# Layer A of a hybrid encoder: the keys of four late blocks selected in one series of small steps, spread over a half pass of the feed-forward

## The chip, the core and the metric

The kernel runs on one core of a Trainium2 chip. The metric is the device time of one execution in microseconds; lower is better. Before the change it is 2746.65 us, the median of 3 runs (2744.76 to 2747.51).

## What is computed

The input is one sequence of 1024 tokens of 1024 values in float32. Layer A is sparse attention with a feed-forward behind it, layer B is attention on a shared latent with a feed-forward behind it. In layer A an indexer scores every key for every token, and a token attends to its 256 best keys (`n_top` is 256 here). Cut to what matters:

```python
score = jnp.einsum('bqh,bqhs->bqs', wib * (IDX_HEADS ** -0.5), jax.nn.relu(dots))
score = jnp.where(admiss[None], score, NEG)
_, idx = lax.top_k(score, n_top)
...
logits = jnp.einsum('bqhd,bqkd->bhqk', qb, kg) * (A_HEAD_DIM ** -0.5) + bias
p = jax.nn.softmax(jnp.where(valid, logits, NEG))
...
def sq_relu_mlp(h, w_up, w_down):
    return jnp.square(jax.nn.relu(h @ w_up)) @ w_down
```

## The kernel before

The tokens lie in eight blocks of 128 (`tb` 0 to 7). A block sees keys up to its own end, so block `tb` has `(tb + 1) * 128` scores per token. Blocks 0 and 1 have at most 256 keys and need no selection; blocks 2 and 3 are selected early, blocks 4 to 7 late.

**Selection** (`select`, line 427) finds the 256th best score by bits: VectorE counts how many scores of a row reach a candidate threshold (line 442, one `tensor_scalar` with an accumulator for each block), compares the counts with 256 (`ok`, line 444), keeps the candidate where enough scores reach it (`thr`, line 455), and sets the next bit (`cand`, line 453). That is a sign step and 31 bits, 32 rounds for each pair of blocks, then one mask step per block (lines 461 to 467; one of its operations, line 463, runs on GpSimd). Each round of a pair is one step of a list; the steps are dealt out between other work by `weave`.

**The feed-forward** (`mlp`) runs in half passes of four blocks. A half pass has eight chunks of four slices of 128 hidden values. For each slice TensorE does 24 matmuls of 512 columns into `pu` (line 1112); ScalarE applies relu and square in place and casts the high half `hh`; VectorE subtracts to make the low half `hl` (line 86). Then 24 matmuls for each of the four blocks add up in `pd` (line 1182), and VectorE adds `pd` to `res` (line 1183). So a chunk has 192 matmuls, four `hl` and four `res`. The weights are split in the same way: ScalarE casts `uh` and `dh`, GpSimd subtracts for `ul` and `dl`, eight such splits in a chunk. `pu` has four banks, `pd` two buffers.

The first half pass (blocks 1, 3, 0, 2) carries the selection of the late blocks as its `extra` steps, first the pair 4, 5 and then the pair 6, 7 (`more` in `layer_a`). After it comes the attention of the blocks 7, 4, 5, 6, then the second half pass with those blocks, whose `extra` steps prepare the down projections of layer B (`down_weights`).

**What sets the order.** Every engine runs its instructions in the order in which a scheduler has placed them, by times that it estimates. An extra step is only kept behind an anchor: `behind` puts its instructions after a given one on the same engine. In `mlp` the anchors are those of the last transposition of the input:

```python
                anchors = turn(late[-1])
            ...
            weave(sum((chunk(c) for c in range(1, NC)), []), extra(st), lambda e: self.behind(e, anchors))
```

**The start.** `bias_table` (line 402) makes a row of position biases for each head, `brow`, and writes it 128 times to memory in `near_d`, from which the attention loads its bias tiles. `brow` lies in the tag `rel`, a ring of three buffers in which also the squares of the norm, the one-hot table, `kvt`, `kiw` and then the normalised keys `k2` (cast `k`, line 271) follow each other. The gain row of the norm has a buffer of its own, tag `gain`, which the scratch of the early selection takes over.

Of the kernel before, what the change touches and what calls it, by code (L numbers as in the profile page):

```python
# [10 lines left out]
F32 = mybir.dt.float32  # L11
F32R = mybir.dt.float32r
U32 = mybir.dt.uint32
AF = mybir.ActivationFunctionType
ALU = mybir.AluOpType
# [3 lines left out]
P = 128  # L19
# [23 lines left out]
class Trunk:  # L43
# [83 lines left out]
    def layer_a(self, res):  # L127
# [4 lines left out]
        with ExitStack() as st_a:  # L132
# [12 lines left out]
            with ExitStack() as st_p:  # L145
# [66 lines left out]
                def load_q(c):  # L212
                    ws["q", c] = weights(256 * c, 256, f"q{c}")

                ws = {}
                with ExitStack() as st_i:
# [114 lines left out]
                    near_d = self.bias_table(i2, pp)  # L331
# [21 lines left out]
                    for tb in (2, 3):  # L353
# [8 lines left out]
                          woven(early[2] + turns[2] + early[3], queries + [lambda: load_q(2)]), sel[:28])  # L362
# [11 lines left out]
                def start(turn):  # L374
                    steps = [lambda c=c, tp=tp: project_q(c, tp) for tp in (0, 2) for c in (2, 3)]
                    weave(steps[:2] + [turn] + steps[2:], sel[28:])
                    st_x.close()
# [5 lines left out]
            def more(st):  # L383
                sp = st.enter_context(tc.tile_pool(name="asel", bufs=2))
                scratch = [self.select_scratch(sp, T, "4", bufs=1)]
                return self.select((4, 5), score, sp, scratch) + self.select((6, 7), score, sp, scratch)
# [15 lines left out]
    def bias_table(self, bp, pp):  # L402
# [11 lines left out]
        row = bp.tile([16, 384], F32, name="brow", tag="rel", bufs=3, padded_shape=[16, T])  # L414
# [9 lines left out]
    def select(self, tbs, score, pool, scratch):  # L424
# [14 lines left out]
        def count():  # L439
            for j, tb in enumerate(tbs):  # L440
                s = score[tb]
                nc.vector.tensor_scalar(scratch[0][0][:, :s.shape[-1]], s, cand[:, j:j + 1], None, op0=ALU.is_ge, op1=ALU.add,  # L442
                                        accum_out=cnt[:, j:j + 1])
            nc.vector.tensor_scalar(ok, cnt, TOP, None, op0=ALU.is_ge)

        def sign():
            nc.vector.memset(cand, 0.0)
            count()
            nc.vector.tensor_copy(thr.bitcast(U32), bits[:, 32:33].to_broadcast([P, n]))
            nc.vector.copy_predicated(thr, ok, cand)  # L450

        def bit(b):
            nc.vector.tensor_tensor(cand.bitcast(U32), thr.bitcast(U32), bits[:, b:b + 1].to_broadcast([P, n]), op=ALU.bitwise_xor)
            count()
            nc.vector.copy_predicated(thr, ok, cand)

        def mask(j):
            s = score[tbs[j]]
            S = s.shape[-1]
            rank, g = (x[:, :S] for x in scratch[0])  # L460
            nc.vector.tensor_scalar(g, s, thr[:, j:j + 1], None, op0=ALU.is_gt, op1=ALU.add, accum_out=cnt[:, j:j + 1])
            nc.vector.tensor_scalar(need[:, j:j + 1], cnt[:, j:j + 1], -BIG, TOP * BIG, op0=ALU.mult, op1=ALU.add)
            nc.gpsimd.tensor_scalar(g, g, BIG, -BIG, op0=ALU.mult, op1=ALU.add)
            nc.vector.tensor_scalar(s, s, thr[:, j:j + 1], BIG, op0=ALU.is_equal, op1=ALU.mult)
            nc.vector.tensor_tensor_scan(rank, s, s, 0.0, ALU.add, ALU.bypass)
            nc.vector.scalar_tensor_tensor(rank, rank, need[:, j:j + 1], s, op0=ALU.is_le, op1=ALU.mult)
            nc.vector.tensor_add(s, rank, g)

        return [sign] + [lambda b=b: bit(b) for b in range(30, -1, -1)] + [lambda j=j: mask(j) for j in range(n)]
# [594 lines left out]
    def mlp(self, layer, res, tbs, finish, done, out=None, extra=lambda st: [], side="left"):  # L1064
# [12 lines left out]
        with ExitStack() as st:  # L1077
# [37 lines left out]
            with tc.tile_pool(name=f"ms{nm0}", bufs=2, side=side) as sp:  # L1115
# [41 lines left out]
                anchors = turn(late[-1])  # L1157
# [44 lines left out]
            weave(sum((chunk(c) for c in range(1, NC)), []), extra(st), lambda e: self.behind(e, anchors))  # L1202
# [48 lines left out]
```

## Time and profile before

| | us |
|---|---|
| median of 3 runs | 2746.65 (2744.76 to 2747.51) |
| the profiled execution | 2747.70 |
| its span | 2745.90 |
| TensorE busy | 2563.0 (93%) |
| VectorE busy | 1574.5 (57%) |
| ScalarE busy | 1236.6 (45%) |
| GpSimd busy | 1018.6 (37%) |

The profile is of one execution. Its engines are PE (TensorE; PEld is its weight loads), DVE (VectorE), ACT (ScalarE), POOL (GpSimd) and SP (which issues the DMAs). PEclk is the granted clock of TensorE as a share of full speed. Where an instruction waited, the row ends with the idle time before it and with what ended the wait.

### The profile page before, as it was taken

What the parts mean: (1) busy time and instruction counts of PE and PEld (TensorE: products, weight loads), DVE (VectorE), ACT (ScalarE), POOL (GpSimd) and SP (SyncE); (2) the same over time, 40 slices, a digit from 0 to 9 for tenths busy, and PEclk for the clock granted to TensorE, in tenths of its full rate; (3) what the DMA queues carried; (4) which work ended last, traced back from release to release, by engine and by line L of the source; (5) the groups of instructions that cost most, each with busy time, mean ns of one, the idle gap of its engine ahead of it and who ended that gap; (6) DMA issues with size and microseconds to landing.
All of it is one profiled execution on the core that took longest, in us unless ns stands there. A gap on an engine that the chain in (4) does not pass through costs nothing.

```text
span 2745.9 us, 37099 instructions
## 1 busy us (share of the span) xinstructions
PE 2563.0 (93%) x13354; PEld 2165.7 (79%) x13354; DVE 1574.5 (57%) x3888; ACT 1236.6 (45%) x2989; POOL 1018.6 (37%) x756
## 2 busy tenths in 40 slices
PE   6798888989999999999989799999999999999999
PEld 5697777767777887888879688887778888888887
DVE  5598768999729885111236888888532232222223
ACT  3476653322328764324235688888422222122221
POOL 1235643443527534435321555555212212122220
PEclk9898999999999999999999899999999999999999
DMA  6211332221323214323220000001401111111111
GB/s 145 46 40 43 92 97 77 92 92 62 108 85 91 61 42 152 110 79 123 75 60 4 12 13 9 14 7 41 138 16 46 47 46 50 43 62 42 51 46 62
DMA packets 122295, 173.05 MB, mean 63 GB/s; under 512 B 12752, under 2 KB 101104, under 8 KB 122112
## 3 DMA queue, kind: packets, MB, share of 16 engines
q1 hardware_dynamic: 122112, 170.69, 20.2%
q8 instruction: 105, 1.72, 0.3%
q14 instruction: 78, 0.64, 0.1%
HBM read 159.13 MB, written 11.53 MB: 62 GB/s over the span
## 4 chain that ended last, share of the span: by engine, by line
PE 69%; DVE 17%; DMA 4%; ACT 4%; POOL 2%; issue 2%; SPq 0%; POOLq 0%; ACTq 0%; DVEq 0%
PE pd L1182 23%; PE pu L1112 21%; DVE both L442 4%; PE pwo L1058 4%; PE blps L930 2%; PE pwoa L1058 2%; PE bpo L954 2%; PE puq L788 2%; PE pq L183 2%; PE po L566 2%; PE ppt L560 1%; PE lps L537 1%; PE bpt L949 1%; DMA near_d<-brow 1%; PE pukv L744 1%
## 5 line engine op out<-in xcount | busy, mean ns | idle before, releaser
L86 POOL TENSOR_TENSOR dl<-rd,dh 128x1024 fp32r<-128x1024 f32 x96 | 231.2, 2417 | 754.3 <-ACT dh L86 384.9
L1183 DVE TENSOR_TENSOR res<-res,pd 128x1024 f32<-128x1024 f32 x192 | 234.4, 1221 | 417.4 <-PE pd L1182 417.4
L1182 PE MATMUL pd<-dh,hl 128*128 128x512 f32 x1024 | 397.1, 394 | 28.5 <-DVE hl L86 28.5
L1112 PE MATMUL pu<-mxh,uh 128*128 128x512 f32 (+1 forms) x1056 | 408.5, 387 | 2.4 <-DVE mxl L86 2.4
L1112 PE MATMUL pu<-mxh,ul 128*128 128x512 f32 (+1 forms) x1056 | 407.8, 386 | 0.0
L1112 PE MATMUL pu<-mxl,uh 128*128 128x512 f32 (+1 forms) x1056 | 407.6, 386 | 0.0
L1182 PE MATMUL pd<-dh,hh 128*128 128x512 f32 x1024 | 399.8, 391 | 5.4 <-ACT hh L86 4.5
L1182 PE MATMUL pd<-dl,hh 128*128 128x512 f32 x1024 | 399.9, 391 | 0.0
L86 ACT CAST dh<-rd 128x1024 fp32r<-128x1024 f32 x96 | 99.1, 1052 | 483.5 <-PE pd L1182 424.7
L86 DVE TENSOR_TENSOR hl<-pu,hh 128x512 fp32r<-128x512 f32 (+1 forms) x132 | 88.8, 674 | 388.0 <-ACT hh L86 388.0
L86 POOL TENSOR_TENSOR ul<-ru,uh 128x1024 fp32r<-128x1024 f32 x96 | 232.2, 2421 | 177.6 <-ACT uh L86 154.1
L1169 ACT ACTIVATE pu<-pu 128x512 f32<-128x512 f32 (+1 forms) x132 | 75.1, 569 | 456.8 <-PE pu L1112 451.3
L1182 PEld LDWEIGHTS pd<-dh,hl 128*128 128x128 f32 x1024 | 193.8, 190 | 72.1 <-DVE hl L86 32.1
L1112 PEld LDWEIGHTS pu<-mxh,uh 128*128 128x128 f32 x1056 | 201.5, 191 | 42.5 <-DVE mxl L86 2.9
L1112 PEld LDWEIGHTS pu<-mxh,ul 128*128 128x128 f32 x1056 | 201.4, 191 | 39.7
L1112 PEld LDWEIGHTS pu<-mxl,uh 128*128 128x128 f32 x1056 | 201.0, 190 | 39.5
L1182 PEld LDWEIGHTS pd<-dh,hh 128*128 128x128 f32 x1024 | 193.2, 189 | 47.2 <-ACT hh L86 5.7
L1182 PEld LDWEIGHTS pd<-dl,hh 128*128 128x128 f32 x1024 | 193.2, 189 | 40.0
L442 DVE TENSOR_SCALAR_CACHE_REDUCE both<-score,cand 128x384 f32<-128x384 f32 (+2 forms) x192 | 181.3, 944 | 4.8
L936 POOL TENSOR_SCALAR bpr<-bpr,bsm 128x640 f32<-128x640 f32 (+7 forms) x128 | 97.7, 768 | 110.7 <-DVE bsm L935 33.3
L548 POOL TENSOR_SCALAR lg<-lg,sm 128x256 f32<-128x256 f32 (+7 forms) x128 | 98.9, 781 | 65.4 <-DVE sm L547 43.1
L86 ACT CAST uh<-ru 128x1024 fp32r<-128x1024 f32 x96 | 99.9, 1044 | 27.4 <-DMA ru<-in_mlp_w_up_dram 26.4
(384 smaller groups left out, 6062.9 us busy)
## 6 DMA issues: line engine op xcount, KB each, us to landing
ru<-in_mlp_w_up_dram SPq DMA_DIRECT2D x48, 1024.0 KB, 5.5
rd<-in_mlp_w_down_dram SPq DMA_DIRECT2D x48, 1024.0 KB, 4.9
bm<-near_d SPq DMA_DIRECT2D x56, 256.0 KB, 2.8
res<-in_x_dram SPq DMA_DIRECT2D x16, 512.0 KB, 5.3
wor_a<-in_a_w_o_dram SPq DMA_DIRECT2D x16, 512.0 KB, 3.7
wr_q<-in_a_w_in_dram SPq DMA_DIRECT2D x8, 512.0 KB, 3.8
x<-res SPq DMA_DIRECT2D x8, 512.0 KB, 2.6
wor_b<-in_b_w_o_dram SPq DMA_DIRECT2D x8, 512.0 KB, 3.7
```

The lines of the kernel that those rows point to most:

```text
L86: return self.nc.scalar.copy(h, src), (engine or self.nc.vector).tensor_sub(l, src, h)
L183: nc.tensor.matmul(out, a[x][:, kb, t0:t0 + P], b[:, kb, :], start=(kb == 0 and i == 0), stop=(kb == KB - 1 and i == 2))
L442: nc.vector.tensor_scalar(scratch[0][0][:, :s.shape[-1]], s, cand[:, j:j + 1], None, op0=ALU.is_ge, op1=ALU.add, accum_out=cnt[:, j:j + 1])
L548: nc.gpsimd.tensor_scalar(lg[:, :S], lg[:, :S], rs, 1.0, op0=ALU.mult, op1=ALU.mult)
L566: nc.tensor.matmul(po, vv[:, s0 + u], m[:, u], start=(s0 + u == 0 and n == 0), stop=(s0 + u == nb - 1 and n == 1))
L788: nc.tensor.matmul(ps[:, 192 * u:192 * u + 192], a[:, kb, tsl], b[:, kb], start=(kb == 0 and i == 0), stop=(kb == 2 and i == 2))
L936: nc.gpsimd.tensor_scalar(pr, pr, sm[:, 3:4], 1.0, op0=ALU.mult, op1=ALU.mult)
L1058: nc.tensor.matmul(open_ps[n], x[:, kb], w[:, kb, ns], start=(kb == 0 and i == 0), stop=(kb == KB - 1 and i == 2))
L1112: nc.tensor.matmul(pu, a[:, kb], b[:, kb, c0:c1], start=(kb == 0 and i == 0), stop=(kb == KB - 1 and i == 2))
L1169: nc.scalar.activation(pu, pu, AF.Relu)
L1182: nc.tensor.matmul(pd[:, ns], a[:, tsl], b[:, ns], start=(f == 0 and k == 0), stop=(f == NS - 1 and k == 2))
L1183: nc.vector.tensor_add(res[:, tb], res[:, tb], pd)
```

## The change

`select` no longer makes one step of a round but one of each count: a step is one bit of one block. The last block's step also makes `ok` and `thr`, the first block's the next `cand`. A mask is three steps. The four late blocks are one series, in the order 7, 4, 5, 6, so that `ok`, `thr` and `cand` are made once for four blocks; a sixth as many empty steps are added behind, so that the series ends ahead of the half pass. `mlp` ties an extra step to `self.tail`, the newest `hh` and `hl`, instead of to the transposition. The early selection of blocks 2 and 3 has the same steps in halves. And `brow` moves from the ring `rel` to the buffer `gain`.

```diff
-                    near_d = self.bias_table(i2, pp)
+                    near_d = self.bias_table(i2, pp, ip)
...
-                          woven(early[2] + turns[2] + early[3], queries + [lambda: load_q(2)]), sel[:28])
+                          woven(early[2] + turns[2] + early[3], queries + [lambda: load_q(2)]), sel[:56])
...
-                    weave(steps[:2] + [turn] + steps[2:], sel[28:])
+                    weave(steps[:2] + [turn] + steps[2:], sel[56:])
...
-                return self.select((4, 5), score, sp, scratch) + self.select((6, 7), score, sp, scratch)
+                steps = self.select((7, 4, 5, 6), score, sp, scratch)
+                return steps + [lambda: None] * (len(steps) // 6)
...
-        row = bp.tile([16, 384], F32, name="brow", tag="rel", bufs=3, padded_shape=[16, T])
+        row = rp.tile([16, 384], F32, name="brow", tag="gain", bufs=1, padded_shape=[16, D])
...
+        def bit(b, j):
+
+            if j == 0 and b < 0:
+                nc.vector.memset(cand, 0.0)
+                nc.vector.tensor_copy(thr.bitcast(U32), bits[:, 32:33].to_broadcast([P, n]))
+            elif j == 0:
+                nc.vector.tensor_tensor(cand.bitcast(U32), thr.bitcast(U32), bits[:, b:b + 1].to_broadcast([P, n]), op=ALU.bitwise_xor)
+            count(j)
+            if j == n - 1:
+                nc.vector.tensor_scalar(ok, cnt, TOP, None, op0=ALU.is_ge)
+                nc.vector.copy_predicated(thr, ok, cand)
...
-        return [sign] + [lambda b=b: bit(b) for b in range(30, -1, -1)] + [lambda j=j: mask(j) for j in range(n)]
+        steps = [lambda b=b, j=j: bit(b, j) for b in (-1, *range(30, -1, -1)) for j in range(n)]
+        return steps + [lambda j=j, part=part: mask(j, part) for j in range(n) for part in range(3)]
...
-                anchors = turn(late[-1])
+                self.tail = turn(late[-1])
...
-            weave(sum((chunk(c) for c in range(1, NC)), []), extra(st), lambda e: self.behind(e, anchors))
+            weave(sum((chunk(c) for c in range(1, NC)), []), extra(st), lambda e: self.behind(e, self.tail))
```

**On VectorE, in the first half pass.** `hl0_1_c_f` is the low half of slice f of chunk c, `score4` to `score7` are the scores of the late blocks. Before, from `hl` of slice 3 of chunk 1 on:

```order
L86 TENSOR_TENSOR hl0_1_1_3_5043<-pu0_1_1_3_0_5044,hh0_1_1_3_5042 128x512
L442 TENSOR_SCALAR both4_4872,cnt4_4875<-score5_80,cand4_4874 128x768
L444 TENSOR_SCALAR ok4_4876<-cnt4_4875 128x2
L455 COPY_PREDICATED thr4_4873<-ok4_4876,cand4_4874 128x2
L453 TENSOR_TENSOR cand4_4874<-thr4_4873,bits_67 128x2
L442 TENSOR_SCALAR both4_4872,cnt4_4875<-score4_79,cand4_4874 128x640
```

Four more rows like these, the rest of another round, follow ahead of the next `hl`. Now, from `hl` of slice 3 of chunk 3 on:

```order
L86 TENSOR_TENSOR hl0_1_3_3_5654<-pu0_1_3_3_0_5655,hh0_1_3_3_5653 128x512
L451 TENSOR_TENSOR cand7_4874<-thr7_4873,bits_67 128x4
L442 TENSOR_SCALAR both4_4872,cnt7_4875<-score7_82,cand7_4874 128x1024
L442 TENSOR_SCALAR both4_4872,cnt7_4875<-score4_79,cand7_4874 128x640
L442 TENSOR_SCALAR both4_4872,cnt7_4875<-score5_80,cand7_4874 128x768
L442 TENSOR_SCALAR both4_4872,cnt7_4875<-score6_81,cand7_4874 128x896
L86 TENSOR_TENSOR hl0_1_4_0_5832<-pu0_1_4_0_0_5833,hh0_1_4_0_5831 128x512
L454 TENSOR_SCALAR ok7_4876<-cnt7_4875 128x4
```

A round now counts four blocks and has its three small operations once, over four columns; rounds are cut by the `hl` of the feed-forward, and the series runs from chunk 1 into chunk 6, where the pairs ran from chunk 0 into chunk 5.

**On ScalarE, at the start.** `k_0` and `k_1` are the two halves of the normalised keys, `wr_qi_0_797` is the third load for the indexer; in brackets stand the semaphores waited for. Before, the first cast of the keys waited for the DMA that reads `brow`:

```order
L305 CAST qs__529<-pqi_256_530 64x256
L271 CAST k_0_524<-krow_508 128x4x64 [waits DMAHW3_49,DVE_49]
L271 CAST k_0_524<-krow_508 128x4x64
L247 COPY kiw<-pkv_445 72x512 [waits PE_49]
L248 CAST kih<-pkv_445 64x512
```

Now it waits for an earlier DMA, that of the one-hot table, and stands ahead of the second `kvt`; the cast of the third load still stands ahead of the second half of the keys:

```order
L271 CAST k_0_524<-krow_508 128x4x64 [waits DMAHW1_49,DVE_49]
L271 CAST k_0_524<-krow_508 128x4x64
L244 COPY kvt<-pkv_445 128x512 [waits PE_49]
L304 CAST qs__529<-pqi_256_530 64x256 [waits PE_49]
```

```order
L264 ACTIVATE ksq_596<-krow_597 128x256 [waits Activation_49]
L86 CAST wh_qi_796<-wr_qi_0_797 128x8x128 [waits DMAHW4_49]
L304 CAST qs__529<-pqi_256_646 64x256 [waits PE_49]
L305 CAST qs__529<-pqi_256_646 64x256
L271 CAST k_1_613<-krow_597 128x4x64 [waits DVE_49]
```

The last five rows read the same in both orders.

## Rows read from the trace of the kernel before

**Rows 1.** The page, part 1: busy time, share of the span, instructions.

```profile
PE 2563.0 (93%) x13354; PEld 2165.7 (79%) x13354; DVE 1574.5 (57%) x3888; ACT 1236.6 (45%) x2989; POOL 1018.6 (37%) x756
```

**Rows 2.** Windows, the two half passes: start:end length, busy us (instructions), clock, DMA.

```profile
core 0: us, PE busy (x) PEld busy (x) DVE busy (x) ACT busy (x) POOL busy (x), PEclk, DMA share, GB/s
425.70:815.50 389.80, 357.80 (x1534) 292.02 (x1532) 314.98 (x544) 115.05 (x162) 155.05 (x67) 0.96 0.25 84
1056.00:1403.80 347.80, 343.44 (x1534) 284.27 (x1533) 78.81 (x83) 122.72 (x179) 148.61 (x62) 1.00 0.30 100
```

**Rows 3.** Waits of TensorE, 425.7 to 815.5: us in total, times, longest.

```profile
PE pd L1182 <- DVE hl L86: 28.5, 7, 8.1
```

**Rows 4.** Windows, one chunk of each half pass.

```profile
522.00:575.00 53.00, 49.41 (x213) 40.50 (x212) 50.69 (x88) 14.72 (x20) 23.68 (x10) 0.97 0.25 80
1111.00:1154.00 43.00, 43.00 (x191) 35.61 (x190) 7.29 (x8) 14.49 (x20) 18.57 (x9) 1.00 0.31 100
```

**Rows 5.** Timeline of ScalarE at the start: start, length, instruction [idle before <-releaser].

```profile
73.94 0.71 ACT L271 CAST k<-krow 128x256 fp32r<-128x256 f32 x2 [18.12 <-DMA near_d<-brow]
...
79.45 0.37 ACT L86 CAST vv<-pk 128x256 fp32r<-128x256 f32 x1
...
89.00 0.71 ACT L271 CAST k<-krow 128x256 fp32r<-128x256 f32 x2 [2.96 <-DVE krow L268]
```

**Rows 6.** DMA issues, 30 to 90: count, KB each, us to landing.

```profile
near_d<-brow SPq DMA_DIRECT2D x1, 3072.0 KB, 34.2
...
wr_qi<-in_a_w_in_dram SPq DMA_DIRECT2D x1, 512.0 KB, 4.0
```

**Rows 7.** Windows, the end of the start.

```profile
66.00:92.00 26.00, 10.34 (x57) 8.96 (x56) 9.03 (x22) 11.50 (x22) 8.02 (x4) 0.64 0.48 89
```

**Rows 8.** Timeline of VectorE, one round where no split runs.

```profile
456.96 0.88 DVE L442 TENSOR_SCALAR_CACHE_REDUCE both<-score,cand 128x640 f32<-128x640 f32 x1
...
457.88 1.01 DVE L442 TENSOR_SCALAR_CACHE_REDUCE both<-score,cand 128x768 f32<-128x768 f32 x1
...
458.94 0.17 DVE L444 TENSOR_SCALAR ok<-cnt 128x2 uint32<-128x2 f32 x1
459.14 0.16 DVE L455 COPY_PREDICATED thr<-ok,cand 128x2 f32<-128x2 uint32 x1
```

**Rows 9.** Lines by form, VectorE, 425 to 800: count | busy us, mean ns | idle.

```profile
L442 DVE TENSOR_SCALAR_CACHE_REDUCE both<-score,cand 128x1024 f32<-128x1024 f32 x32 | 40.9, 1277 | 0.8
L442 DVE TENSOR_SCALAR_CACHE_REDUCE both<-score,cand 128x896 f32<-128x896 f32 x32 | 36.6, 1145 | 1.0
...
L442 DVE TENSOR_SCALAR_CACHE_REDUCE both<-score,cand 128x768 f32<-128x768 f32 x32 | 32.4, 1011 | 1.0
L444 DVE TENSOR_SCALAR ok<-cnt 128x2 uint32<-128x2 f32 x64 | 31.3, 489 | 1.5
L455 DVE COPY_PREDICATED thr<-ok,cand 128x2 f32<-128x2 uint32 x62 | 29.5, 475 | 2.1
L442 DVE TENSOR_SCALAR_CACHE_REDUCE both<-score,cand 128x640 f32<-128x640 f32 x32 | 28.1, 879 | 1.0
...
L453 DVE TENSOR_TENSOR cand<-thr,bits 128x2 uint32<-128x2 uint32 x62 | 25.0, 403 | 2.1
```

**Rows 10.** Timeline of GpSimd, VectorE and ScalarE at 492: a round that meets a split.

```profile
492.01 2.41 POOL L86 TENSOR_TENSOR dl<-rd,dh 128x1024 fp32r<-128x1024 f32 x1 [1.99 <-ACT dh L86]
...
492.46 1.99 DVE L444 TENSOR_SCALAR ok<-cnt 128x2 uint32<-128x2 f32 x1
...
494.01 0.59 ACT L86 CAST hh<-pu 128x512 fp32r<-128x512 f32 x1
```

**Rows 11.** Lines, GpSimd, 425.7 to 725: the splits.

```profile
L86 POOL TENSOR_TENSOR ul<-ru,uh 128x1024 fp32r<-128x1024 f32 x25 | 61.4, 2460 | 52.1 <-ACT uh L86 51.8
L86 POOL TENSOR_TENSOR dl<-rd,dh 128x1024 fp32r<-128x1024 f32 x25 | 60.8, 2445 | 107.4 <-ACT dh L86 107.4
```

**Rows 12.** Line 442, all counts: min/median/max ns, first and last start in us.

```profile
L442 DVE TENSOR_SCALAR_CACHE_REDUCE both<-score,cand x192: 604/942/1282, 122.2 to 713.7; 128x384 f32<-128x384 f32 x32, 128x512 f32<-128x512 f32 x32, 128x640 f32<-128x640 f32 x32, 128x768 f32<-128x768 f32 x32
```

**Rows 13.** Timeline of TensorE: the transposes of the second half of the keys.

```profile
65.90 0.60 PE L257 MATMUL pk<-ident,kvt 128*128 128x128 f32 x4
```

More of the change, by code (lines that the diff above doesn't have):

```diff
@@ L400, in gain_qk, with bias_table @@
         return gk
-    def bias_table(self, bp, pp):
+    def bias_table(self, bp, pp, rp):
         nc, tc = self.nc, self.tc
@@ L437, in select, with count, mask @@
         bits = self.bits
[L439 to L457, printed above, removed]
+        def count(j):
+            s = score[tbs[j]]
+            nc.vector.tensor_scalar(scratch[0][0][:, :s.shape[-1]], s, cand[:, j:j + 1], None, op0=ALU.is_ge, op1=ALU.add,
+                                    accum_out=cnt[:, j:j + 1])
+        def bit(b, j):
[8 more added lines that the diff above has]
+                nc.vector.copy_predicated(thr, ok, cand)
+        def mask(j, part):
             s = score[tbs[j]]
@@ L460, in mask @@
             rank, g = (x[:, :S] for x in scratch[0])
[L461 to L467, printed above, removed]
-        return [sign] + [lambda b=b: bit(b) for b in range(30, -1, -1)] + [lambda j=j: mask(j) for j in range(n)]
+            if part == 0:
+                nc.vector.tensor_scalar(g, s, thr[:, j:j + 1], None, op0=ALU.is_gt, op1=ALU.add, accum_out=cnt[:, j:j + 1])
+                nc.vector.tensor_scalar(need[:, j:j + 1], cnt[:, j:j + 1], -BIG, TOP * BIG, op0=ALU.mult, op1=ALU.add)
+                nc.gpsimd.tensor_scalar(g, g, BIG, -BIG, op0=ALU.mult, op1=ALU.add)
+                nc.vector.tensor_scalar(s, s, thr[:, j:j + 1], BIG, op0=ALU.is_equal, op1=ALU.mult)
+            elif part == 1:
+                nc.vector.tensor_tensor_scan(rank, s, s, 0.0, ALU.add, ALU.bypass)
+            else:
+                nc.vector.scalar_tensor_tensor(rank, rank, need[:, j:j + 1], s, op0=ALU.is_le, op1=ALU.mult)
+                nc.vector.tensor_add(s, rank, g)
+        steps = [lambda b=b, j=j: bit(b, j) for b in (-1, *range(30, -1, -1)) for j in range(n)]
+        return steps + [lambda j=j, part=part: mask(j, part) for j in range(n) for part in range(3)]
     def attend_a(self, tbs, res, kh, kl, vv, score, edge, near_d, wst, lp=None, start=None, beside=None, free=None):
```

## The prediction, made before the changed kernel ran

> **What bounds the kernel now.** I read the page first, then the stretches, then single lines. The page has TensorE busy for 93% of the span and VectorE for 57% [rows 1], so TensorE bounds the whole, and the question is where it is held up. Two stretches matter here. The first is the first half pass of layer A's feed-forward. The two half passes of it do the same matmuls (1534 in each stretch), so one prices the other: from the last split of the input to the last addition the first takes 389.8 us and the second 347.8 us, at a granted clock of 0.96 and 1.00 [rows 2]. The reader is to see that the difference, 42.0 us, is the most that any new order of the first half pass can give, unless it went faster than the second one, where TensorE is busy 343.4 of 347.8 us. In the first, VectorE is busy 315.0 of 389.8 us against 78.8, and what TensorE waits for is `hl`, the low half of the hidden values, which VectorE makes: 28.5 us in seven waits [rows 3]. A chunk (192 matmuls) shows it: VectorE is busy 50.7 of 53.0 us while a chunk of the second half pass takes some 43 us, with 7.3 us of VectorE [rows 4]. So here VectorE is the bound, and the selection of keys is its load.
>
> The second stretch is the start. ScalarE stands still for 18.1 us until the write of `near_d` has landed, before it can cast the normalised keys `k`; `near_d` takes 34.2 us [rows 5, 6]. In the 26 us from 66 to 92 TensorE is busy for 10.3 us, at a clock of 0.64 [rows 7].
>
> **Part 1: the series of four blocks.** Removed: per bit there was an `ok`, a `thr` and a `cand` for two blocks at a time, 64 triples; now there is one triple for all four, 32. The counts stay: 32 for each block. Their price is start to start in a quiet stretch: 0.92 us for 640 columns, 1.06 for 768, and 0.20 for each small operation [rows 8]. That is 0.04 to 0.05 us over the means, 0.88 and 1.01 us [rows 9], so I take 1.19 and 1.33 us for 896 and 1024 columns (means 1.15 and 1.28). A bit of four blocks is 4.50 + 0.60 = 5.1 us where nothing disturbs it.
>
> The small operations are not always 0.17 us: when GpSimd runs a split of weights (2.4 us) they last until it ends. At 492.0 the first of two such splits begins, and an `ok` right behind it takes 1.99 us [rows 10]; the counts stay at their 0.88 and 1.01 us. Over the stretch the small ones average 0.489, 0.475 and 0.403 us [rows 9]: over 0.165 us that is 64 x 0.32 + 62 x 0.31 + 62 x 0.24 = 54.6 us of holding, or 0.85 us per triple, or 54.6 / 50 = 1.09 us per split (25 + 25 until the selection ends at 725) [rows 11].
>
> Now the load of a chunk. The 140 steps and 23 empty ones are dealt over 84 steps of the feed-forward, 12 to a chunk: 23.3 counts, 5.8 bits, 29.7 us. The chunk's own four `hl` and four `res` are 7.3 us [rows 4]. Holding is not in any row for bits of this length; by the triple it is 5.8 x 0.85 = 5.0 us, by the split 8 x 1.09 = 8.8 us. These are the two ends. I take the triple: a split holds something only if a triple comes while it runs, and a triple now comes every 43.5 / 5.8 = 7.5 us instead of every 288 / 64 = 4.5. So 29.7 + 7.3 + 5.0 = 42.0 us of VectorE in a chunk that TensorE needs 347.8 / 8 = 43.5 us for. It fits, barely, in six chunks (the first has no selection, the last next to none).
>
> Fitting on average is not enough, since each engine takes its instructions in order. In the new order one to two thirds of a bit, at most 6.5 us, stands between two of the feed-forward's instructions. By the order on TensorE, which the change hardly moves here, an `hl` is used some 37 matmuls (37 x 43.5 / 192 = 8.4 us) after the last matmul that it comes from; three operations of ScalarE take 1.8 us of that [rows 10], `hl` itself 0.7, so 5.9 us are left; a `res` has 26 matmuls, 5.9 us less its own 1.2, before its bank of `pd` is wanted again. Holding adds 2 to 3 us at one place. I leave 2 us for lateness in all. **The half pass gives 42.0 - 2 = 40 us.**
>
> Edits with one answer: the masks are twelve steps instead of four, the same instructions, four of them on GpSimd of about 1 us, each waiting for a count of VectorE and holding the next split behind it; the loads run a chunk ahead, so nothing. The counts end in the seventh chunk, not at 714 [rows 12]; the attention that uses the masks starts behind the last chunk, at 815, and needs block 7, which is now the first masked: nothing. In the second half pass the eight steps on layer B's down projections are tied to the newest `hl`: eight loads on SP, each behind a load of `w_up` and with a wait for the step before (a chunk earlier), 16 casts and 16 subtractions. VectorE is busy 78.8 of 347.8 us there [rows 2], the last step has four `down` of 5.4 us ahead of the end: nothing; without that cover one load of 4 us and some 2 us of casts. The steps for blocks 2 and 3 at 120 to 330 are cut finer, with the same instructions: nothing, give or take 4 us of another order.
>
> **Part 2: `brow` in the gain's buffer.** The cast of `k` now waits for an old load instead of `near_d`. `near_d` itself is issued where it was, after the last scaling of the input; who waits for it next is the first count of blocks 2 and 3, at 122 [rows 12], and it lands at about 74: no new wait of any size. What is late next is the second half of the keys: in the trace 9.6 us pass from its first cast (79.45) to its cast of `k` (89.00) [rows 5]. Its transposes end at 66.5 [rows 13], so 76 is the earliest, 13 us sooner. But on ScalarE a cast of the third load of `w_in` for the indexer stands ahead of it. That load is now issued while `near_d` still moves; if it goes behind it, it lands at 73.9 + 4.0 [rows 6], and 1.8 us of casts later the cast of `k` runs at about 80: 9 us sooner. No row shows two such transfers together; I take the later, **9 us**, with 13 as the other end and nothing as the low one.
>
> **The sum.** The profiled execution took 2747.7 us for a span of 2745.9. 2747.7 - 40 - 9 = 2698.7; the median of the three runs is 1.05 us lower, so **2698 us** (rounded; the rivals below are given the same way). Less than 0.2%, 5.5 us, can't be told from no change.
>
> **A rule beside it.** The Trainium skill (SBUF — State Buffer, "Who interferes with whom") has VectorE and GpSimd share a pair of ports, held for a whole instruction by whichever starts first; a `tensor_scalar` that writes its accumulator out is exempt. The trace agrees with both halves: `ok` ends with the split, the counts don't wait. By that rule a small operation that comes at a random moment waits half a split times the share of time in which splits run, and that speaks against this change; the first rival carries the price.
>
> **The rivals.**
> 1. VectorE stays the bound. Small operations come at random: splits fill 8 x 2.45 = 19.6 of 43.5 us, so each waits 0.45 x 1.22 = 0.55 us, 17.5 of them 9.6 us; by the split it was 8.8. With 8.8 a chunk needs 45.8 us, 2.3 too many, six times: the half pass gives 28 us, the time is 2709; with 9.6 it is 2714. For it: the load is within 4% of the chunk. Against: the trace holds 0.28 us per operation, half of that.
> 2. The start gives nothing, since ScalarE waits for the third load as it did for `near_d`: 2707. For it: one queue carries both. Against: the load would have to land at 87.
> 3. Slower: VectorE's chunk grows past 52. Then six chunks lose the 49 us again, (52.0 - 43.5) x 6 = 51. That takes 15.0 us of holding, 1.88 us per split. If every split held VectorE for its full 2.45 us, a chunk would take 37.0 + 19.6 = 56.6 us, the half pass 79 us more than the second, and the kernel 2774 us. For it: the two splits at 492 came back to back, and such a pair can hold two of a triple. Against: 1.09 us is what splits cost at twice as many triples.
> 4. More: both parts reach their ends, 42 + 13, and the stage behind gains a little from its order: about 2690.
>
> **How the numbers follow.** My forecast gets 0.60, rival 1 0.18, rival 2 0.10, rival 3 0.04, rival 4 0.08. Predicted is the likeliest, 2698. The range goes down to 2685 (rival 4 with the 4 us of order) and up to 2716 (rival 1 with some of 2's loss); rival 3 and part of 1 with 2 together lie outside. Faster 0.95, within 5.5 us 0.02 (VectorE's chunk at about 52), slower 0.03.
>
> **What would show it.** From the last split of the input to the last addition the first half pass takes about 350 us; VectorE is 95% busy or more in its chunks two to seven but TensorE's waits for `hl` fall from 28.5 to under 5 us; `ok`, `thr` and `cand` come 32 times at about 0.4 to 0.5 us. The wait of ScalarE on `near_d` is gone, and the second cast of `k` is near 80. Wrong would be: waits for `hl` or `res` of over 10 us in all, chunks of over 45 us, a cast of weights that waits 10 us for its load, or a stage between 120 and 420 that is longer by what the start won.

## The result, and the profile after

The changed kernel takes 2698.73 us, the median of 4 runs (2695.57 to 2701.47), against 2745.7 us of the kernel before beside it: a ratio of 0.9826, 95% interval 0.9811 to 0.9841. Forecast were 2698 us, in a range from 2685 to 2716. The profiled execution took 2697.45 us for a span of 2695.6 us, 50.3 us less than the span of before.

The page, part 1, and the two half passes of the feed-forward (windows: start:end length, busy us (instructions) of each engine, clock, DMA share, GB/s). They answer to [rows 1] and [rows 2]:

```profile
PE 2541.9 (94%) x13354; PEld 2154.4 (80%) x13354; DVE 1525.8 (57%) x3791; ACT 1235.1 (46%) x2989; POOL 1017.5 (38%) x756
```

```profile
419.22:772.27 353.05, 345.54 (x1534) 285.27 (x1532) 270.90 (x448) 115.55 (x162) 156.64 (x67) 1.00 0.28 93
1014.09:1358.99 344.90, 343.10 (x1534) 284.34 (x1532) 78.26 (x83) 122.24 (x179) 147.87 (x62) 1.00 0.30 101
```

The reader is to see three things. The first half pass went from 389.8 to 353.05 us with the same 1534 matmuls; the second lost 2.9 us too, where nothing was expected; and the granted clock of the first rose from 0.96 to 1.00. From the last split to the last addition, 425.64 to 815.54 and 419.22 to 772.27 us, the gain is 36.85 us. Of it 24.5 us are idle time of TensorE (389.90 - 357.86 = 32.0 before, 353.05 - 345.54 = 7.5 now), and 12.3 us are the same matmuls being busy for less at the higher clock. What TensorE still waits for there (waits, 419.2 to 772.3; [rows 3] before):

```profile
PE pd L1186 <- DVE res L1187: 3.2, 1, 3.2
PE pd L1186 <- DVE hl L86: 1.7, 1, 1.7
PE pd L1186 <- ACT hh L86: 1.4, 1, 1.4
```

Of 28.5 us for `hl` in seven waits 1.7 us are left in one. Three of the chunks (windows, [rows 4] before):

```profile
513.00:557.00 44.00, 42.30 (x187) 34.71 (x186) 42.91 (x70) 13.42 (x19) 18.64 (x8) 1.00 0.29 96
600.00:643.00 43.00, 43.00 (x191) 35.63 (x190) 39.12 (x73) 14.74 (x20) 18.83 (x9) 1.00 0.29 98
687.00:730.00 43.00, 39.81 (x168) 32.16 (x167) 38.85 (x48) 13.57 (x19) 25.18 (x11) 0.96 0.30 98
```

VectorE is busy for 42.9 of 44 us and then for less. TensorE runs without a gap in the second window; the first holds the wait of 1.7 us for `hl`, the third that of 3.2 us for `res`. The operations of the selection (lines by form, VectorE, 420 to 780; [rows 9] before):

```profile
L442 DVE TENSOR_SCALAR_CACHE_REDUCE both<-score,cand 128x1024 f32<-128x1024 f32 x32 | 40.9, 1279 | 1.1
...
L454 DVE TENSOR_SCALAR ok<-cnt 128x4 uint32<-128x4 f32 x32 | 21.4, 667 | 0.9
...
L455 DVE COPY_PREDICATED thr<-ok,cand 128x4 f32<-128x4 uint32 x32 | 11.7, 367 | 1.0
...
L451 DVE TENSOR_TENSOR cand<-thr,bits 128x4 uint32<-128x4 uint32 x31 | 9.9, 318 | 1.0
```

The counts cost what they did. The three small ones went from 31.3 + 29.5 + 25.0 (and 2.5 of the sign step) to 43.0 us; over 0.165 us for each of the 95 that is 27.3 us of holding, 0.85 us per triple. That is a mean over unequal cases. At 518 us three splits in a row hold one operation each (timeline of VectorE):

```profile
518.52 2.29 DVE L454 TENSOR_SCALAR ok<-cnt 128x4 uint32<-128x4 f32 x1
520.84 2.33 DVE L455 COPY_PREDICATED thr<-ok,cand 128x4 f32<-128x4 uint32 x1
523.20 2.32 DVE L451 TENSOR_TENSOR cand<-thr,bits 128x4 uint32<-128x4 uint32 x1
```

With the three counts ahead of them and the one behind, 11.5 us of selection stand between two `hl` there (515.4 to 526.8 us), and the second of these is the one that TensorE waits 1.7 us for.

The start (timeline of ScalarE, then the DMA issues from 30 to 90; [rows 5, 6] before):

```profile
47.34 0.71 ACT L271 CAST k<-krow 128x256 fp32r<-128x256 f32 x2 [3.50 <-DVE krow L268]
...
77.53 1.04 ACT L86 CAST wh_qi<-wr_qi 128x1024 fp32r<-128x1024 f32 x1 [9.78 <-DMA wr_qi<-in_a_w_in_dram]
...
79.24 0.71 ACT L271 CAST k<-krow 128x256 fp32r<-128x256 f32 x2
```

```profile
near_d<-brow SPq DMA_DIRECT2D x1, 3072.0 KB, 34.3
...
wr_qi<-in_a_w_in_dram SPq DMA_DIRECT2D x1, 512.0 KB, 12.1
```

The wait for `near_d` is gone. The third load takes 12.1 us beside that write instead of 4.0, ScalarE waits 9.8 us for it, and the second cast of `k` comes at 79.24 instead of 89.00.

Where the 50.3 us came from, and the same stretches in the runs below (us; each from one profile but the median; the profile of before is that of 2747.7 us):

| kernel | second cast of `k` | last split | half pass | second half pass | from its end to the end | median of runs |
|---|---|---|---|---|---|---|
| before | 89.0 | 425.6 | 389.9 | 347.8 | 1342.1 | 2745.7 |
| changed | 79.2 | 419.2 | 353.1 | 344.9 | 1336.6 | 2698.7 |
| changed, once more | 81.0 | 421.0 | 352.8 | 344.9 | 1336.4 | 2697.4 |
| 1 bias row alone | 79.2 | 422.4 | 394.8 | 349.5 | 1336.1 | 2744.3 |
| 2 without it | 88.1 | 422.6 | 353.4 | 344.9 | 1340.8 | 2701.1 |
| 3 fixed tie | 79.2 | 418.7 | 381.5 | 349.6 | 1339.4 | 2733.2 |
| 4 two pairs | 79.6 | 418.6 | 385.5 | 344.9 | 1340.9 | 2731.0 |
| 5 no late selection | 80.7 | 420.8 | 345.7 | 344.9 | 1338.3 | 2691.4 |
| 6 no empty steps | 79.2 | 419.9 | 358.2 | 344.9 | 1340.0 | 2701.5 |
| 7 denser | 79.9 | 421.7 | 370.9 | 344.9 | 1334.6 | 2723.9 |
| 8 write late | 74.6 | 420.0 | 352.9 | 344.9 | 1338.7 | 2695.5 |
| 9 write in halves | 73.3 | 412.8 | 352.8 | 344.9 | 1341.0 | 2693.6 |
| 10 and masks apart | 74.6 | 414.0 | 352.1 | 344.9 | 1335.2 | 2690.8 |
| 11 and from the first chunk | 74.8 | 413.9 | 351.5 | 344.9 | 1337.4 | 2690.7 |

The medians are of 4 runs, of 10 for the bias row alone and 5 for the last. So of the 50.3 us 6.4 stand at the last split, 36.9 are the half pass, 2.9 the second half pass, 5.5 the stage behind, and the attention between gave back 1.3. Differences of 2 to 3 us in the first two columns say little by themselves: six of these profiles (changed, once more, 4, 5, 6 and 7) have one and the same order on the four compute engines up to the last split, and there the cast lies between 79.2 and 81.0 us and the last split between 418.6 and 421.7.

### The profile page after: what moved, and what is told of

The parts are those of the page before. It is cut to its first block, busy times and chain, and to the rows that moved or that the text cites. A ratio compares the mean times of both kernels' runs of the same rounds, so it can differ in the third digit from the quotient of the medians.

```text
span 2695.6 us, 36994 instructions
## 1 busy us (share of the span) xinstructions
PE 2541.9 (94%) x13354; PEld 2154.4 (80%) x13354; DVE 1525.8 (57%) x3791; ACT 1235.1 (46%) x2989; POOL 1017.5 (38%) x756
## 4 chain that ended last, share of the span: by engine, by line
PE 55%; DVE 4%; ACT 2%; DMA 1%; issue 1%; POOL 1%; SPq 0%; DVEq 0%; ACTq 0%; POOLq 0%
PE pu L1116 20%; PE pd L1186 19%; PE pwo L1062 3%; PE blps L934 3%; PE bpo L958 2%; PE puq L792 2%; PE bpt L953 1%; PE pukv L748 1%; PE pcq L851 1%; PE pck L851 1%; DVE bpr L935 1%; ACT bpr L938 1%; PE pwob L1062 0%; DVE bpl L86 0%; PE pqt L823 0%
## 5 line engine op out<-in xcount | busy, mean ns | idle before, releaser
L442 DVE TENSOR_SCALAR_CACHE_REDUCE both<-score,cand 128x1024 f32<-128x1024 f32 (+1 forms) x192 | 181.2, 944 | 4.5
L550 ACT ACTIVATE lg<-lg,sm 128x256 f32<-128x256 f32 (+7 forms) x128 | 99.4, 778 | 33.7 <-DVE sm L546 30.4
```

The source lines that it names most:

```text
L550: nc.scalar.activation(lg[:, :S], lg[:, :S], AF.Exp, bias=mn, scale=-1.0, accum_out=sm)
```

## The experiments

**1 and 2. The bias row alone, and all but it.** The edit of `brow` in the kernel before, and taken out of the changed one:

```diff
-        row = bp.tile([16, 384], F32, name="brow", tag="rel", bufs=3, padded_shape=[16, T])
+        row = rp.tile([16, 384], F32, name="brow", tag="gain", bufs=1, padded_shape=[16, D])
```

> The kernel before with one edit of the change: the bias row in the gain's buffer. Theory (the start and the half pass are independent terms): the second cast of the keys comes at about 79 us as in the changed kernel, 9.8 us sooner than before, the half pass stays at 390 us, and the time is 2745.7 - 9.8 = 2736 us if nothing behind gives it back. Rival (the 3.3 us that the changed kernel lost between 110 and 420 us belong to the early start itself): last split of the input at about 419 us and 2739 us. If the theory holds, the last split is at about 416 us, and the 3.3 us belong to the finer cut of the early selection.

> The changed kernel with the bias row back in the ring of three. Theory: the cast of the keys waits 18 us for the write of the bias table again, the half pass stays at 353 us, and the time is 2698.7 + 9.8 = 2708.5 us at most, 2705 if the stage up to 420 us takes back what it lost. Rival (the half pass gains only because it starts sooner): half pass over 360 us.

The row alone: 2744.3 us, ratio 0.9987 (0.9974 to 1.0000), 3 us instead of 9.8, which is neither the theory's 2736 us nor the rival's 2739. All but the row: 2701.1 us, 0.9829 (0.9808 to 0.9851), under the 2705 to 2708.5 us expected and by its ratio not to be told from the whole change. The second theory held for the half pass (353.4 us) and the first fell: neither 416 nor 419 us, but 422.4 at the last split. The cast came 9.8 us sooner and the last projection of queries still ended 9.7 us sooner, at 290.9 instead of 300.6 us. The loss is behind it, in the attention of the first four blocks. Windows from that end to the last split, of before, of the row alone, of the changed kernel and of all but the row:

```profile
300.60:425.64 125.04, 107.60 (x584) 87.29 (x583) 80.46 (x282) 74.41 (x192) 62.37 (x68) 0.95 0.33 100
```

```profile
290.90:422.44 131.54, 111.35 (x593) 92.41 (x592) 80.97 (x283) 74.46 (x193) 62.48 (x68) 0.91 0.30 95
```

```profile
290.90:419.22 128.32, 106.82 (x593) 87.96 (x592) 80.98 (x281) 74.75 (x193) 62.31 (x68) 0.96 0.31 97
```

```profile
299.10:422.59 123.49, 106.15 (x583) 86.14 (x583) 79.90 (x280) 74.12 (x192) 62.55 (x68) 0.96 0.33 101
```

Where the row moved, the stretch takes 128 to 132 us, where it did not 123 to 125. Up to the last split the instructions are the same, but the scheduler, whose estimate of the start moved, placed them in another order (so some nine matmuls more fall behind the last projection: 593 against 584). In the changed kernel the outputs of several heads (`po`) stand between the scores of the next block, and TensorE waits 2.64 us before a transposition of queries:

```profile
296.48 0.60 PE L564 MATMUL ppt<-ident,lg 128*128 128x128 f32 x4
299.72 0.68 PE L513 MATMUL ptq<-identr,qt 128*128 128x128 f32 x4 [2.64 <-DVE pl L86]
```

In the kernel without the row the same place reads

```profile
303.72 0.40 PE L541 MATMUL lps<-kl,qst 128*128 128x512 f32 x1
304.00 0.53 PE L513 MATMUL ptq<-identr,qt 128*128 128x128 f32 x4
```

That this order costs the time is inferred; no run had the early start with the old order. But it shows in every profile: TensorE is idle for 20 to 23 us of this stretch in the twelve with the row moved and for 17 in the two without, so some 4 us go with the order. The rest goes with the granted clock, which lies between 0.91 (the row alone) and 0.97 in this stretch of the twelve. Experiment 9 agrees: where the start moves by another 6 us and the stretch stays at 128.7 us, the gain arrives.

The half pass of 394.8 us with the row alone is 4.9 more than before, although the small steps stand in the same order there. It is the one with VectorE as its bound: VectorE is busy for 319.2 us instead of 315.1, since `cand` takes 29.3 us instead of 25.0, and the waits for `hl` are 33.5 us instead of 28.5. So in the same order the splits held more; why they met the small operations otherwise stays open.

**3 and 4. One part of the new selection at a time.** The tie of the steps to the transposition again; and two series of two blocks instead of one of four:

```diff
-                self.tail = turn(late[-1])
+                anchors = self.tail = turn(late[-1])
...
-            weave(sum((chunk(c) for c in range(1, NC)), []), extra(st), lambda e: self.behind(e, self.tail))
+            weave(sum((chunk(c) for c in range(1, NC)), []), extra(st), lambda e: self.behind(e, anchors))
```

```diff
-                steps = self.select((7, 4, 5, 6), score, sp, scratch)
+                steps = self.select((7, 4), score, sp, scratch) + self.select((5, 6), score, sp, scratch)
```

> The changed kernel, but the small steps in the feed-forward stay tied to the last transposition of the input instead of to the newest low half. By the order that the scheduler makes of it, the counts begin in the first chunk and end at the start of the sixth, 28 to 29 in a chunk instead of 23. Theory (what counts is VectorE's load of a chunk against 43.5 us): 28.5 counts are 7.1 bits, 7.1 x (5.1 + 0.85) + 7.3 = 49.5 us, 6 us too many in five chunks, so the half pass takes about 380 us and the kernel some 2725 us; waits for hl of 15 to 25 us. Rival A (the number of triples alone decides): half pass at 353 us, 2699 us. Rival B (the spread alone decides): back at 390 us, 2735 us.

> The changed kernel, but two series of two blocks each (7 and 4, then 5 and 6) instead of one of four; small steps, empty steps and ties as in the change. Theory (load of a chunk): 23.3 counts are 25 us, 11.7 triples 7.0 us and 10 us of holding by the triple or 8.8 by the split, and 7.3: 48 to 49.5 us, 5 to 6 us too many in six chunks, half pass about 385 us, kernel about 2731 us. Rival B (the spread alone decides): 353 us and 2699 us.

Measured: 381.5 us for the half pass and 2733.2 us (0.9949, 0.9931 to 0.9968) with the fixed tie; 385.5 us and 2731.0 us (0.9941, 0.9920 to 0.9961) with pairs. Both half passes came within 2 us of what the load of a chunk gave (380 and 385), and both rivals that give all to one part fell. The kernel with the fixed tie, however, is 8 us over the 2725 of the theory and near the 2735 of rival B, though its half pass is not at 390; 4.7 of the 8 us are its second half pass, see below. And the load was met as a sum, not in each term: holding was 1.31 us per triple with the fixed tie ((57.7 - 95 x 0.165) / 32) and 1.00 with pairs ((95.6 - 190 x 0.165) / 64) instead of 0.85, and with the fixed tie the 128 counts took 232.5 us, 27 in 49 us instead of 28 to 29. Waits of TensorE over the half pass and a window of about a chunk (TensorE gets through 181 and 157 of a chunk's 192 matmuls), fixed tie first, then pairs:

```profile
PE pd L1186 <- DVE hl L86: 22.7, 9, 7.2
```

```profile
518.00:567.00 49.00, 43.94 (x181) 35.48 (x180) 47.74 (x77) 13.56 (x19) 18.22 (x8) 0.93 0.26 86
```

```profile
PE pd L1186 <- DVE hl L86: 24.4, 9, 7.8
```

```profile
513.00:557.00 44.00, 37.99 (x157) 30.86 (x156) 42.57 (x75) 13.58 (x19) 18.60 (x8) 0.92 0.30 96
```

VectorE has no room, and the waits of before come back. Fewer triples without the spread give 8.4 us of the half pass, the spread without fewer triples 4.4; together they give 36.9, because only together do they bring a chunk under TensorE's 43.5 us. The fixed tie shows a second thing: its second half pass takes 349.6 us, as it does with the row alone, while every kernel with the new tie has 344.9. The steps there are the down projections of layer B. Waits of TensorE in the second half pass, and ScalarE at 1076 us, in the kernel before:

```profile
PE pd L1182 <- ACT hh L86: 3.1, 2, 2.6
```

```profile
1076.42 0.96 ACT L678 ACTIVATE whk<-wrk,gc_k 128x288 fp32r<-128x288 f32 x2 [1.90 <-DMA wrk<-in_w_dkv_dram]
1077.29 0.56 ACT L86 CAST hh<-pu 128x512 fp32r<-128x512 f32 x1
```

and the waits of the changed one:

```profile
PE pd L1186 <- ACT hh L86: 0.5, 1, 0.5
```

With the fixed tie the scheduler pulled those steps to the front, and ScalarE waited for their loads ahead of an `hh` that TensorE needed (in experiment 3 TensorE waits 3.1 us for ScalarE in that pass). Tied to the newest `hl`, they stand later.

**5. The ceiling.** The steps of the late selection left out:

```diff
-                return steps + [lambda: None] * (len(steps) // 6)
+                return []
```

> The changed kernel with the selection of the four late blocks left out (no counts and no masks of blocks 4 to 7, so their attention uses unmasked scores). Theory (the 353.1 us of the half pass hold 3.2 + 1.7 us of waits for VectorE and little else): half pass at 347 to 349 us, and with the attention as it was 2693 to 2696 us. Rival (the loads, GpSimd or ScalarE hold the first half pass as well): half pass stays over 351 us.

Half pass 345.7 us, kernel 2691.4 us (0.9798, 0.9782 to 0.9814): a little below both expectations, and the rival fell. Window of the half pass and all waits of TensorE in it:

```profile
420.82:766.52 345.70, 343.07 (x1534) 284.35 (x1532) 62.59 (x67) 115.72 (x162) 147.95 (x63) 1.00 0.28 95
PE pd L1186 <- ACT hh L86: 1.4, 1, 1.4
```

So the selection still costs 7.4 us in the half pass, and without it that pass is within 0.8 us of the second one.

**6 and 7. Less and more in a chunk.** No empty steps behind the selection, or half as many as there are steps:

```diff
-                return steps + [lambda: None] * (len(steps) // 6)
+                return steps
```

```diff
-                return steps + [lambda: None] * (len(steps) // 6)
+                return steps + [lambda: None] * (len(steps) // 2)
```

> The changed kernel without the empty steps: 20 counts in a chunk instead of 23, the masks in the last chunk. Theory (load of a chunk): 5 x 5.95 + 7.3 = 37 us in chunks two to seven, so the two waits in the middle (1.7 and 3.2 us) go; but the masks of four blocks, about 32 us of VectorE, now lie with 7.3 us of the last chunk's own and stand ahead of its additions, so up to 4 us come back there: 2695 to 2701 us. Rival (the end of the selection close to the attention costs more): the attention waits for its masks, over 2705 us.

> The changed kernel with half as many empty steps as steps (a sixth before): 30 counts in a chunk, the selection done in under five chunks. Theory (load of a chunk): 7.5 x 5.95 + 7.3 = 52 us, 8.5 us too many in 4.7 chunks, 40 us: half pass about 393 us, kernel about 2739 us. Rival (lateness is small anyway, since the steps stand in small portions between the low halves): under 2715 us.

Less: 358.2 us and 2701.5 us (0.9826, 0.9809 to 0.9842). The time is just over the expected range, and the reasons are others than expected: `hl` is waited for five times, 7.2 us, about 1 us in each of four chunks and 3.0 in the last. (The ratio is that of the changed kernel all the same: the attention between the half passes, in an order of its own, took 237.2 us there and 240 to 243 in all the others.) With 20 counts in a chunk a triple lies in the same place of each. Timelines of VectorE and GpSimd there:

```profile
652.10 1.97 DVE L454 TENSOR_SCALAR ok<-cnt 128x4 uint32<-128x4 f32 x1
654.10 2.32 DVE L455 COPY_PREDICATED thr<-ok,cand 128x4 f32<-128x4 uint32 x1
656.46 2.31 DVE L451 TENSOR_TENSOR cand<-thr,bits 128x4 uint32<-128x4 uint32 x1
...
660.00 0.69 DVE L86 TENSOR_TENSOR hl<-pu,hh 128x512 fp32r<-128x512 f32 x1
```

```profile
651.64 4.76 POOL L86 TENSOR_TENSOR dl<-rd,dh 128x1024 fp32r<-128x1024 f32 x2 [1.97 <-ACT dh L86]
656.35 2.40 POOL L86 TENSOR_TENSOR ul<-ru,uh 128x1024 fp32r<-128x1024 f32 x1
```

Three splits in a row hold the three small operations, one each, 6.6 us where 0.5 would do, and the `hl` behind them is late, as once in the changed kernel. So the load of a chunk is not the whole rule: where triple and splits fall counts as well. Over the half pass a triple is held for 1.44 us here (30.0 + 18.2 + 13.6 = 61.8 us, less 95 x 0.165, over 32), against 0.85 in the changed kernel.

Denser: 370.9 us and 2723.9 us (0.9901, 0.9885 to 0.9917) where 393 and 2739 were expected. The direction is the theory's, the size about half of it; the profile is of the fastest of the four runs, 2715.2 us, where the others took 2723 to 2725, so their half pass may have been longer. The window over the five chunks concerned:

```profile
470.00:712.00 242.00, 231.17 (x995) 189.18 (x993) 231.93 (x395) 77.92 (x108) 103.63 (x45) 0.98 0.28 92
```

VectorE is 96% busy, so it is the bound (TensorE waits 9.2 us for `hl` in the half pass, and once, 5.1 us, for a split of GpSimd); but the 128 counts run from 447.2 to 684.2 us, 237 us, not 4.3 chunks of 52. The scheduler placed them later than they were dealt out, so a chunk held some 25 of them, not 30.

**8 and 9. The write of the bias table.** Behind the third load, all of it or its second half:

```diff
-        nc.sync.dma_start(near.rearrange("h (c r) -> h c r", c=P), row.unsqueeze(1).to_broadcast([16, P, 384]))
-        return near
+        def write(c0):
+            nc.sync.dma_start(near.rearrange("h (c r) -> h c r", c=P)[:, c0:c0 + 64], row.unsqueeze(1).to_broadcast([16, 64, 384]))
+
+        write(0)
+        return near, lambda: write(64)
...
-                    near_d = self.bias_table(i2, pp, ip)
+                    near_d, write = self.bias_table(i2, pp, ip)
...
+                    self.behind(write, [self.load])
```

> The changed kernel, with the write of the bias table issued behind the third load of w_in for the indexer instead of ahead of it. In the changed kernel ScalarE waited 9.8 us for that load, which took 12.1 us beside the write. Theory: the load lands at about 70 us, the second cast of the keys comes at about 72 instead of 79, but the write now lands at about 100, and the first loads for the queries, whose cast would come at 97, stand behind it: they land at 104 to 108, so most of the 7 us is given back: 2692 to 2701 us. Rival (the loads share the queue without loss): all 7 us stay, 2691 us.

> The changed kernel, with the write of the bias table in two halves, the first where it was, the second behind the third load of w_in for the indexer. Theory: the first half lands at about 59 us, the load at about 70, the second half at about 87, before the casts of the query weights at about 97 need theirs: the second cast of the keys comes at about 72 instead of 79 and the 7 us stay: about 2692 us. Rival (the write takes as long for half as many repeats): the load waits as before, 2699 us.

All of it: 2695.5 us (0.9807, 0.9793 to 0.9822), with the cast of `k` at 74.6 us; then a cast of query weights waits 5.5 us, the last split comes at 420.0, and most is given back, as the theory had it. In halves: 2693.6 us (0.9795, 0.9780 to 0.9810), the cast at 73.3 us. DMA issues from 30 to 95 and ScalarE's cast of the third load:

```profile
near_d<-brow SPq DMA_DIRECT2D x2, 1536.0 KB, 18.1
wr_q<-in_a_w_in_dram SPq DMA_DIRECT2D x2, 512.0 KB, 16.2
wr_qi<-in_a_w_in_dram SPq DMA_DIRECT2D x1, 512.0 KB, 3.9
```

```profile
69.36 1.04 ACT L86 CAST wh_qi<-wr_qi 128x1024 fp32r<-128x1024 f32 x1 [1.59 <-DMA wr_qi<-in_a_w_in_dram]
```

A half takes 18.1 us, the load between the halves 3.9, and ScalarE's wait of 9.8 us is 1.6. The last split comes 6.5 us sooner than in the changed kernel. It is the write that the load had waited behind.

**10, 11 and the changed kernel once more.** On top of 9, an empty step behind each mask step; then also the steps dealt over all eight chunks:

```diff
+                rest = [lambda: None] * (len(steps) // 6)
+                return steps[:-12] + sum(([s, rest.pop()] for s in steps[-12:]), []) + rest
```

```diff
-            for step in chunk(0):
-                step()
-            weave(sum((chunk(c) for c in range(1, NC)), []), extra(st), lambda e: self.behind(e, self.tail))
+            weave(sum((chunk(c) for c in range(NC)), []), extra(st), lambda e: self.behind(e, self.tail))
```

> The kernel with the bias table in two halves, and in the half pass one empty step behind each mask step, the other eleven at the end. Theory: the wait for res of 3.2 us, which came from a run of mask operations ahead of it, goes; half pass at 350 us, the kernel 3 us under the one with the halves alone, about 2691 us. Rival (the wait moves to the next addition or low half): 2693 us or more.

> As the one before, and the steps are dealt over all eight chunks instead of the last seven, with a fifth as many empty steps: 21 counts in a chunk instead of 23, and the first chunk carries some. Theory (load of a chunk): 5.25 x 5.95 + 7.3 = 38.5 us of VectorE, so the 1.7 us wait for hl goes too: half pass 348 to 350 us, kernel about 2690 us. Rival (the splits, which come in the same place of each chunk, hold a triple ahead of a low half, as in the kernel without empty steps, 1 us in a chunk): half pass 353 to 358 us, 2694 to 2699 us.

> The changed kernel once more, on the chip of the three kernels beside it, so that they can be compared: 2695 to 2702 us; the stage behind the layer, which was 5.5 us shorter in its first profile than in that of the kernel before, by the theory (that part is scatter between executions) comes out between 1335 and 1342 us from the last addition of the second half pass to the end; by the rival (the change shortened it) at 1337 us again.

2690.8 us (0.9792, 0.9776 to 0.9807), 2690.7 us (0.9789, 0.9774 to 0.9804) and 2697.4 us (0.9821, 0.9805 to 0.9837) beside the same runs of before. Both are faster than the changed kernel by some 7 us, but that is the write in halves: experiment 9 alone has a ratio of 0.9795, and the half passes of 352.1 and 351.5 us gain 1 us where 3 were expected. So the 2691 and 2690 us of the two theories came out, and not for their reason. Of the waits that the masks apart were to remove, 2.5 us for `res` and 2.3 for `hl` remain, so the rival of 10, a wait that moves on, is right for the half pass. Of 11 neither theory is: 3.4 us for `hl`.

The stage behind the second half pass took 1336.4 us the second time, 1336.6 the first. That lies in the range of the theory and at the number of the rival, so the run does not decide between them. The other profiles say more. The order of the instructions in that stage goes with the row: the two kernels without the moved row have one order (1342.1 and 1340.8 us), all the others have different ones. But eight profiles with the very same order there on the four compute engines (changed, once more, 1, 3, 4, 5, 7 and 8) lie between 1334.6 and 1340.9 us. Scatter between executions is thus as large as the 5.5 us; whether the order adds to it is not shown.

## Why the prediction was right

Sign, mechanism and most single steps came out; that the total did to within 1 us is luck. The half pass and the start gave 36.9 us and, at the last split, 6.4 us where 40 and 9 were forecast; 2.9 and 5.5 us, less 1.3, came from places that stood at nothing.

- **The half pass (40 us)** gave 36.9 in the profile. The mechanism is shown: with the load of a chunk back over TensorE's time (3, 4, 7) the waits for `hl` are back, with it taken away (5) they are gone. The price of holding, 0.85 us per triple, was met to the second digit (27.3 / 32 = 0.85), though other orders show 1.44 (6), 1.31 (3) and 1.00 (4), so it is a price of this order and no constant. The choice of the triple over the split was right: 45 splits ran between 452 us and the last triple, 0.61 us each, not 1.09. The 3 us short of 40 are the term for lateness, 2 us in the sum: the half pass is 5.3 us over the 347.8 us it was priced by. I had one to two thirds of a bit between two of the feed-forward's instructions, at most 6.5 us, with holding of 2 to 3; in the trace a whole bit can stand there (the order printed under "The change" has four counts between two `hl` too), 11.5 us at 515 us with some 6.4 of holding, and TensorE waits 1.7 us for the `hl` behind it. The largest single wait is 3.2 us for a `res` behind a run of mask operations, which I had costed at nothing for their place.
- **The start (9 us)** was right to the point where I stopped: `k` at 79.24 us, forecast 80, for the reason given (third load behind `near_d`). The step that failed is that this gain reaches the end because no new wait of any size follows. By experiment 1 it is worth 3.6 us, between nothing and 7 (0.0013 and its interval times 2747), since the attention behind takes 128 to 132 us instead of 123 to 125 in the order the scheduler then makes (that it is the order is inferred). In its profile 3.2 of the 9.8 us are left at the last split; behind it the half passes take 4.9 and 1.7 us more and the last stage 6.0 less, none of which was forecast. My sign for this, a longer stage between 120 and 420 us, did fire, for 3.3 us in the changed kernel. Another, a cast of weights that waits 10 us for its load, came to 9.8 us, but it was no sign of being wrong: a load that lands behind `near_d`, as forecast, makes that wait.
- **The edits at nothing** were not all nothing. The new tie gave 2.9 us in the second half pass, where I asked only what the steps cost when tied later, not what they cost where they stood: the 2.6 us wait behind `whk` was in the trace of before, and no row of mine showed it. That the finer early selection gave anything is not shown: the 3 us at the last split in experiment 2 (422.6 against 425.6) are no more than the 3.1 us by which profiles of one order differ there. The 5.5 us of layer B stood in no term.
- **The rivals.** The first (small operations come at random, 0.55 us each) is refuted for this order: 0.29 us. Its rule in the Trainium skill (SBUF — State Buffer, "Who interferes with whom") stands. Experiment 6 shows it plainest, three splits and three small operations in turn. But the half split for each was an average for chance, and here the order decides. The second fell: the load landed at 77.5 us, not 87. The third did not come, but its mechanism is that of experiment 6, at 1 us a chunk, and of the one wait for `hl` in the changed kernel.
- **Signs that were off.** VectorE was to be 95% busy or more in chunks two to seven; it is 98% in one of the windows and 84 to 94% in the three behind it. The counts run from 444.7 to 699.5 us, 255 us, so 21.9 in 43.5 us and not 23.3: (5.46 x 5.95) + 7.3 = 39.8 us, the mean of the four windows from 513 to 687 us (42.9, 40.6, 39.1, 36.8). Chunks of over 45 us were to mean wrong; from last addition to last addition the second took 46.0 us and the seventh, with the masks, 51.1.

## What to carry to other kernels

Work that is hidden beside another engine is free only while its whole load, its own and what it is held for, fits in each repetition of what it hides behind; here neither the smaller load nor the better spread was worth much alone, and both together nearly all there was. Price an early start to the end and not to the first instruction that it moves: where a scheduler places by estimated times, one buffer can come with another order of a stage 200 us further on, and here a third to two thirds of the gain was gone at its end. And where a tie is changed, look up what the old place of the tied steps costs, not only the new one.

## What was not expected of the hardware

- The operations that the splits hold include those of a mask: in the changed kernel a scan over 1024 columns takes 4.36 us and a `scalar_tensor_tensor` over 640 columns 2.83 us, in experiment 6 the same kinds take 2.29 and 0.89. The scan holds in its turn: the split behind it takes 4.38 us instead of 2.4.
- Two writes of 1536 KB take 18.1 us each where one of 3072 KB takes 34.3, and a load of 512 KB issued while the whole one moves takes 12.1 us instead of 3.9: here cutting the long write cost about 2 us (36.2 against 34.3) and let the short load through.
- The granted clock fell with the waits. In the half pass before it stood at one half (1.2 GHz) six times, for 3.4 to 10.2 us and 34 us in all, each time during or just behind a wait of TensorE of 2.6 to 8.1 us; in the changed kernel once, for 3.4 us, behind the wait of 3.2 us. Windows in the longest of the six, and in the one:

```profile
452.50:462.50 10.00, 5.99 (x14) 4.74 (x15) 9.44 (x28) 0.00 (x0) 0.00 (x0) 0.50 0.09 31
723.10:726.30 3.20, 3.20 (x9) 2.43 (x9) 3.17 (x6) 0.00 (x0) 1.25 (x1) 0.50 0.00 0
```

  Over the half pass that is 1.00 instead of 0.96, a third of what the half pass gained.
